# A second group by seven products in half of the gate and up units, with shared products in the accumulators' banks and 4 KB landing tiles

## The chip, the cores and the metric

The kernel runs on one core of a Trainium2 chip. The metric is the device time of one execution in microseconds. TensorE (PE) multiplies, PEld is its weight load, VectorE (DVE) and ScalarE (ACT) do the elementwise work, GpSimd (POOL) issues a few transfers, and SyncE (SP) issues the large ones.

## The reference

One layer of a decoder block on 256 tokens of width 2048, all in float32:

```
h = h + 0.5 * swiglu(rms_norm(h, ffn1_norm), ffn1_w_gate, ffn1_w_up, ffn1_w_down)
n = rms_norm(h, mix_norm) @ w_in                  # split among retention and sliding-window attention
h = h + concat(retention(n), swa(n)) @ w_out
h = h + memory_cross_attention(rms_norm(h, xa_norm), rms_norm(mem, mem_norm), xa_wq, xa_wkv, xa_wo)
h = h + 0.5 * swiglu(rms_norm(h, ffn2_norm), ffn2_w_gate, ffn2_w_up, ffn2_w_down)
out = rms_norm(h, final_norm)
swiglu(x, g, u, d) = (silu(x @ g) * (x @ u)) @ d   # g, u: 2048 x 5632; d: 5632 x 2048
```

## The kernel before

The 256 tokens are two halves t of 128, which are the rows of a matmul. The hidden width of an FFN, 5632, is 11 blocks b of 512 columns, in three groups (0 to 3, 4 to 7, 8 to 10); after the gate and up blocks of a group comes its part of the down projection. The contraction of 2048 is four groups of 512, each of four slices of 128.

**Precision.** A weight piece of float32 lands by SP's queue in a tile `wf`. ACT copies it into its high half `wh` (line 74), DVE subtracts to get the low half `wl` (line 79), both in fp32r, and PE multiplies three times (`three`, lines 632 to 634): high by high, high by low, low by high. There are four buffers each of `wh` and `wl`. The left operands (`blk`) are split in the same way.

**Units.** `Unit` is a plain product of one block. `Twin` does two outputs together: gate b and up b, or two blocks of a down projection. Three of its four contraction groups are multiplied plainly, in steps of two slices for each output (both token halves: 12 matmuls of 512 columns a step). The fourth group, `seven`, is done by seven products in place of eight, in the manner of Strassen and Winograd: token halves by outputs by halves of the contraction. A product is two slices, 6 matmuls. For it DVE subtracts weights from one another (line 222), four times a Twin, and the left operand needs sums, which `sums_of` makes for gate and up after gate b=0 is done: ACT scales four pieces of h, DVE makes four sums of 256 columns (line 279), and these are split into halves (line 74 on ACT, line 79 on DVE). There are 28 Twins: b=1 to 10 in each FFN and four for the down projections of each.

Before, four of the seven products stand alone in the four `tmp` banks of PSUM and three go into the accumulators `acc` (two tiles of two banks). One product is put behind each of the plain steps 2 to 8 of the Twin's own. DVE then adds products and accumulators in SBUF (`t2k`, line 249, eight adds a Twin).

**Order.** `later(delay, fn)` puts a task in a list by a step counter; `run_due` runs those due ahead of a step. Splits are issued LOOKAHEAD = 3 steps ahead and loads AHEAD = 4 steps before these. A scheduler orders the instructions of an engine, and each engine works in its order. Waits between engines are set by tile. Loads go to five `wf` tiles of 8 KB per partition, mostly 1 MB each.

Of the kernel before, what the change touches and what calls it, by code (L numbers as in the profile page):

```python
# [35 lines left out]
SWA_EVERY = 5  # L36


@with_exitstack
def decoder_block(ctx: ExitStack, tc: tile.TileContext, a: dict, out: bass.AP):  # L40
# [20 lines left out]
    def big(dt=F32):  # L61
        return wpool.tile([P, 2, 1024], dt, tag="wf", name=nm("wf"), bufs=5)
# [95 lines left out]
    class Unit:  # L158
# [4 lines left out]
        def __init__(self, w, index, n, lhs, done, blocks, per_half=False, pair=False):  # L163
            self.w, self.n, self.lhs, self.done = w[2 * index : 2 * index + 2] if pair else w[index], n, lhs, done
            self.blocks, self.per_half, self.pair = list(blocks), per_half, pair
            self.then = None
            units.append(self)

        def steps(self):
# [9 lines left out]
    class Twin:  # L179

        then, n, per_half = None, 512, False

        def __init__(self, weights, lhs, plain, seven, sums, done, pair=True):
            self.w, self.lhs, self.plain, self.seven = weights, lhs, list(plain), seven
            self.sums, self.done, self.pair = sums, done, pair
            self.acc, self.products, self.wide = [None, None], {}, []
            units.append(self)

        def steps(self):
            plain = [(b, f, i) for b in self.plain for f in range(2) for i in range(2)]  # L190
            out = []
            for at, (b, f, i) in enumerate(plain):
                out.append((self, b, range(2 * i, 2 * i + 2), f, b == plain[0][0] and i == 0, b == plain[-1][0] and i == 1))
                if 2 <= at < 9:
                    out.append((self, self.seven, None, at - 2, False, False))
            return out

        def fetch(self, at, steps, loaded):
            _, b, ks, f, _, _ = steps[at]
            if ks is None:  # L200
                return
            other = next(i for i in range(at + 1, len(steps)) if steps[i][2] is not None)
            loaded[at], loaded[other] = load_pair(self.w[f], b) if self.pair else load(self.w[f], 2 * b, 2)
            if b == self.plain[0]:
                self.load_wide(f)

        def load_wide(self, f):
            x, c = big(), self.seven
            if self.pair:
                nc.sync.dma_start(x, self.w[f][:, c].rearrange("f p n -> p f n"))  # L210
                x = x.rearrange("p f (k n) -> p k f n", n=S)
            else:
                nc.sync.dma_start(x, self.w[f][2 * c : 2 * c + 2].rearrange("c p n -> p c n"))
                x = x.rearrange("p c (k f n) -> p (c k) f n", k=2, f=2)
            self.wide.append(x)

        def prepare(self, kind):
            (g0, g1), (u0, u1) = ([x[:, i::2] for i in range(2)] for x in self.wide)
            src = (g0, g1, u1, g0, u0, u1, g1)[kind]
            if kind > 2:  # L220
                p, q = ((u0, g0), (u1, u0), (u1, g0), (g1, u1))[kind - 3]
                nc.vector.tensor_tensor(src, p, q, ALU.subtract)  # L222
            wh, wl = (wpool.tile([P, 1024], F32R, tag=x, name=nm(x)) for x in ("wh", "wl"))
            halves(*(x.rearrange("p (k f n) -> p k f n", k=2, f=2) for x in (wh, wl)), src)
            return [x.rearrange("p (k n) -> p k n", n=512) for x in (wh, wl)]

        def multiply(self, kind, wh, wl):
            x, sums = self.lhs[self.seven], self.sums[self.seven]
            alone = kind in (0, 3, 4, 5)
            if alone:  # L230
                o = self.products[kind] = tmp_ps()
            else:
                o = self.acc[kind == 2][:, int(kind == 6), :]
            for j in range(2):
                if kind in (0, 1, 6):
                    k, t = 2 * j + (kind > 0), int(kind == 6)
                    v = [x[:, k, c, t * P : (t + 1) * P] for c in range(2)]
                else:
                    i = {2: 3, 3: 0, 4: 2, 5: 1}[kind]
                    v = [sums[:, c, i, j, :] for c in range(2)]  # L240
                three(o, *v, wh[:, j, :], wl[:, j, :], alone and j == 0, alone and j == 1)
            if kind == 0:
                later(1.5, self.first_copy)
            if kind == 5:
                later(1, self.first_sums)
                later(2, self.second_sums)

        def add(self, out, a, b):
            nc.vector.tensor_tensor(out, a, b, ALU.add)  # L249
# [1055 lines left out]
```

## Time and profile before

| | before |
|---|---|
| median of 3 runs | 2148.33 us (2145.35 to 2149.93) |
| the profiled execution | 2148.38 us, span 2146.2 us, mean granted clock 0.997 |
| PE | 2129.7 us busy, 99% |
| DVE | 1664.5 us, 78% |
| ACT | 1144.4 us, 53% |
| transfers | 478 issues on SP's queue; 482.50 MB in all, 225 GB/s |

A row of the timeline has the start, the duration, the engine, the line, what is written and read, the shape and the count, and in brackets the idle time before it with what ended it. A matmul's row is longer than its distance from the next, since matmuls overlap. FFN1 ends at about 730 us of the span and FFN2 begins at about 1450 us; between them lie the mixer and the attention over the memory.

### The profile page before, as it was taken

The page shows a single profiled execution, that of the slowest core. Times are in us where ns is not written, and L with a number is a line of the kernel's source. Part 1 is how long each engine was busy: PE and PEld are TensorE (multiplying, and loading weights), DVE is VectorE, ACT ScalarE, POOL GpSimd, SP SyncE. Part 2 cuts the span into 40 slices and gives each one's busy share as a digit, 9 for nine tenths or more (in the row PEclk, how much of TensorE's full clock was granted, in tenths as well). Part 3 has the DMA queues.
Part 4 walks back from the last instruction along what each step waited for, and adds up shares of the span by engine and source line. Part 5 has one row for each costly group of instructions (what it writes and reads, how often), then busy time and mean ns, then how long its engine had stood idle before and what let it go on. Part 6 is the DMA issues. An engine that isn't in the chain of part 4 may idle for free.

```text
span 2146.2 us, 25612 instructions
## 1 busy us (share of the span) xinstructions
PE 2129.7 (99%) x9624; PEld 1764.9 (82%) x9624; DVE 1664.5 (78%) x1984; ACT 1144.4 (53%) x1395; POOL 159.1 (7%) x273
## 2 busy tenths in 40 slices
PE   9999999999999999999999999999999999999998
PEld 7888888888888878888788888888888888888886
DVE  6988888888885778787665555567988888888875
ACT  6555555555554554646455444455655455555554
POOL 0000100001001110101110110010100000000000
PEclk9999999999999999999999999999999999999999
DMA  7767676767657666666776766476876575656663
GB/s 295 238 205 253 233 239 224 246 218 253 230 202 255 216 225 207 204 208 221 251 249 214 241 218 206 156 245 235 250 269 225 178 249 203 233 200 228 205 227 141
DMA packets 138444, 482.50 MB, mean 225 GB/s; under 512 B 11984, under 2 KB 11984, under 8 KB 138192
## 3 DMA queue, kind: packets, MB, share of 16 engines
q1 hardware_dynamic: 125888, 447.26, 59.7%
q0 software_dynamic: 12288, 33.57, 6.7%
q8 instruction: 75, 1.23, 0.2%
q14 instruction: 49, 0.40, 0.1%
q10 hardware_dynamic: 144, 0.05, 0.0%
HBM read 445.17 MB, written 35.65 MB: 224 GB/s over the span
## 4 chain that ended last, share of the span: by engine, by line
PE 57%; DVE 2%; DMA 2%; issue 1%; ACT 0%; POOL 0%; POOLq 0%; ACTq 0%; DVEq 0%
PE acc L633 17%; PE acc L632 17%; PE acc L634 17%; DMA t4k<-box 2%; PE tmp L634 2%; PE tmp L632 2%; PE tmp L633 2%; DVE wl L79 1%; DVE h L647 0%; PE tmp L866 0%; POOL t4k L619 0%; DVE t4k L610 0%; PE tmp L847 0%; DVE blk L520 0%; DMA box<-t4k 0%
## 5 line engine op out<-in xcount | busy, mean ns | idle before, releaser
L74 ACT ACTIVATE wh<-wf 128x1024 fp32r<-128x1024 f32 (+1 forms) x861 | 905.9, 1056 | 884.5 <-PE acc L634 819.5
L79 DVE TENSOR_TENSOR wl<-wf,wh 128x1024 fp32r<-128x1024 f32 (+1 forms) x861 | 1037.9, 1215 | 373.4 <-ACT wh L74 357.6
L632 PE MATMUL acc<-wh,blk 128*128 128x512 f32 (+1 forms) x2832 | 1100.6, 389 | 1.2 <-ACT wh L74 1.2
L633 PE MATMUL acc<-wl,blk 128*128 128x512 f32 (+1 forms) x2832 | 1099.1, 388 | 1.1 <-DVE wl L79 1.0
L634 PE MATMUL acc<-wh,blk 128*128 128x512 f32 (+1 forms) x2832 | 1098.1, 388 | 0.0
L632 PEld LDWEIGHTS acc<-wh,blk 128*128 128x128 f32 x2832 | 533.0, 188 | 112.2 <-ACT wh L74 2.4
L633 PEld LDWEIGHTS acc<-wl,blk 128*128 128x128 f32 x2832 | 533.0, 188 | 109.0 <-DVE wl L79 1.9
L634 PEld LDWEIGHTS acc<-wh,blk 128*128 128x128 f32 x2832 | 532.9, 188 | 108.7
L619 POOL DMA_DIRECT2D t4k<-box x256 | 147.8, 584 | 1772.3 <-DMA box<-t4k 748.4
L222 DVE TENSOR_TENSOR wf<-wf,wf 128x1024 f32<-128x1024 f32 x84 | 102.6, 1222 | 1.9
L632 PE MATMUL tmp<-wh,blk 128*128 128x512 f32 x224 | 87.1, 389 | 0.0
L633 PE MATMUL tmp<-wl,blk 128*128 128x512 f32 x224 | 87.1, 389 | 0.0
L634 PE MATMUL tmp<-wh,blk 128*128 128x512 f32 x224 | 87.1, 389 | 0.0
L249 DVE TENSOR_TENSOR t2k<-t2k,acc 128x512 f32<-128x512 f32 x112 | 71.8, 683 | 9.5 <-PE acc L634 9.5
L249 DVE TENSOR_TENSOR t2k<-t2k,tmp 128x512 f32<-128x512 f32 x112 | 76.5, 684 | 1.9
L610 DVE STREAM_TRANSPOSE t4k<-t2k 128x512 f32<-128x512 f32 x96 | 63.0, 691 | 10.2 <-ACT t2k L74 10.0
L634 PEld LDWEIGHTS tmp<-wh,blk 128*128 128x128 f32 x224 | 42.0, 188 | 8.7
L632 PEld LDWEIGHTS tmp<-wh,blk 128*128 128x128 f32 x224 | 42.0, 188 | 8.7
L633 PEld LDWEIGHTS tmp<-wl,blk 128*128 128x128 f32 x224 | 42.0, 188 | 8.7
L79 DVE TENSOR_TENSOR blk<-t4k,blk 128x512 fp32r<-128x512 f32 (+2 forms) x72 | 44.1, 653 | 4.8 <-ACT blk L74 4.6
L74 ACT ACTIVATE blk<-t4k 128x512 fp32r<-128x512 f32 (+2 forms) x72 | 39.2, 596 | 7.5 <-DMA t4k<-box 7.5
L647 DVE TENSOR_TENSOR h<-h,t4k 128x512 f32<-128x512 f32 x40 | 25.8, 687 | 16.6 <-DMA t4k<-box 16.6
(149 smaller groups left out, 720.1 us busy)
## 6 DMA issues: line engine op xcount, KB each, us to landing
wf<-in_ffn_w_up SPq DMA_DIRECT2D x88, 1024.0 KB, 6.6
wf<-in_ffn_w_down SPq DMA_DIRECT2D x88, 1024.0 KB, 6.9
wf<-in_ffn_w_gate SPq DMA_DIRECT2D x87, 1024.0 KB, 6.9
box<-t4k SPq DMA_DIRECT2D x64, 512.0 KB, 3.3
t4k<-box POOLq DMA_DIRECT2D x256, 128.0 KB, 7.0
wf<-in_w_in_rqk SPq DMA_DIRECT2D x16, 1024.0 KB, 7.4
wf<-in_w_in_rvg SPq DMA_DIRECT2D x16, 1024.0 KB, 5.4
wf<-in_w_out SPq DMA_DIRECT2D x16, 1024.0 KB, 8.0
```

The lines of the kernel that those rows point to most:

```text
L74: return nc.scalar.activation(dst, src, AF.Copy, **kw)
L79: nc.vector.tensor_tensor(lo, src, hi, ALU.subtract)
L222: nc.vector.tensor_tensor(src, p, q, ALU.subtract)
L249: nc.vector.tensor_tensor(out, a, b, ALU.add)
L610: nc.vector.transpose(z[:, t, :].rearrange("p (g q j) -> p q g j", g=4, q=4), squares_of(v))
L619: nc.gpsimd.dma_start(z[32 * g : 32 * g + 32].rearrange("p t (i n) -> p (t i) n", i=4), far[g])
L632: nc.tensor.matmul(o, ah, bh, start=start, stop=False)
L633: nc.tensor.matmul(o, ah, bl, start=False, stop=False)
L634: nc.tensor.matmul(o, al, bh, start=False, stop=stop)
L647: nc.vector.tensor_tensor(v, v, out[t], ALU.add)
```

## The change

`Twin` is written anew.

- `sevens` takes the place of `seven`: for b in DOUBLE = (2, 4, 6, 8, 10) two of the four contraction groups (2 and 3) are done by seven products each, so two plain groups are left; in the other Twins one.
- All products accumulate in the four banks that become the Twin's outputs, the plain steps after them in the same banks. The first, third, fifth Twin of an FFN and so on takes the four `tmp` banks (`spare`), every second one the two `acc` tiles. What two outputs share is copied out of a bank by ACT (`keep`, `keep_other`, `middle`, `spread`: four copies) and added into the banks by DVE (four adds).
- A Twin that is `ahead`, all but the first of an FFN, has its products P1, P5, P6, P3 and P7 inside the preceding unit and P2 and P4 inside its own. The first (b=1) has P1, P5, P6, P3, P2 and P7 ahead of its plain steps.
- After gate b=0 `sums_of` makes the sums of block 3 (delay 1) and of block 2 (delay 8).
- `wf` is ten tiles of 4 KB per partition (`land`), one load of 512 KB each. A load of gate and up pieces brings two runs of 2 KB per partition.
- The tables and keys that lie in such tiles (`dmat`, `box`, `keys`) take two or one of the small ones.

In counts of the two programs: 60 matmuls of 512 columns fewer on PE; on DVE 30 weight splits and 40 subtractions of weights more and net 112 adds of 512 columns fewer; on ACT 30 splits and net 84 pieces of 512 columns more; on SP 863 issues in place of 478.

```diff
+LAND = 10
+DOUBLE = (2, 4, 6, 8, 10)
+P1, P5, P6, P3, P7, P2, P4 = range(7)
-    def big(dt=F32):
-        return wpool.tile([P, 2, 1024], dt, tag="wf", name=nm("wf"), bufs=5)
+    def land(dt=F32):
+        return wpool.tile([P, 1024], dt, tag="wf", name=nm("wf"), bufs=LAND)
...
     class Twin:
+        plan = {
+            P1: ((0, 0), (0, 0), (0, 0)),
+            P5: ((1, 0), (1, 1), 0),
+            P6: ((1, 0), (0, 1), 1),
+            P7: ((0, 0), (0, 1), 2),
+            P2: ((0, 1), (0, 0), (1, 0)),
+            P4: ((0, 1), (0, 1), (1, 1)),
+            P3: ((1, 1), (1, 0), 3),
+        }
...
+        def chunks(self, kinds):
+            return [
+                (self, c, None, kind, c == self.sevens[0], c == self.sevens[-1]) for kind in kinds for c in self.sevens
+            ]
...
+        def bank(self, f, t):
+            if self.spare:
+                if (f, t) not in self.acc:
+                    self.acc[f, t] = tmp_ps()
+                return self.acc[f, t]
+            if f not in self.acc:
+                self.acc[f] = ps_acc.tile([P, 2, 512], F32, tag="acc", name=nm("acc"))
+            return self.acc[f][:, t, :]
...
+            if last and kind in (P1, P5, P6, P7):
+                later(0, {P1: self.keep, P5: self.keep_other, P6: self.middle, P7: self.spread}[kind])
...
+        def keep(self):
+            self.u1 = self.copied(self.bank(0, 0))
+        def keep_other(self):
+            self.p5 = self.copied(self.bank(1, 1))
+        def middle(self):
+            x = self.bank(0, 1)
+            self.add(x, self.u1, x)
+            self.u2 = self.copied(x)
+            self.add(self.p5, self.p5, self.u2)
+        def spread(self):
+            for x, y in ((self.copied(self.bank(0, 1)), self.bank(1, 1)), (self.p5, self.bank(1, 0))):
+                self.add(y, x, y)
...
     def all_steps():
...
+        for (u, x), (after, _) in zip(groups, groups[1:] + [(None, None)]):
+            chunks = []
+            if isinstance(u, Twin):
+                if not u.ahead:
+                    out += u.chunks((P1, P5, P6, P3, P2, P7))
+                chunks = u.chunks((P2, P4) if u.ahead else (P4,))
+            own, n = len(chunks), len(x)
+            if isinstance(after, Twin) and after.ahead:
+                chunks += after.chunks((P1, P5, P6, P3, P7))
+            space = len(chunks) if len(chunks) > own else 2 * own
+            for at, step in enumerate(x):
+                out.append(step)
+                for i, c in enumerate(chunks):
+                    place = (2 * i + 1) * n // (2 * space)
+                    if i < own:
+                        place = min(place, n - 4)
+                    if place == at:
+                        out.append(c)
...
+    def load(w, piece):
+        wf = land()
+        if len(w.shape) == 3:
+            nc.sync.dma_start(wf, w[piece])
+            return wf
+        src = w[:, piece // 2, :, 512 * (piece % 2) : 512 * (piece % 2) + 512].rearrange("f p n -> p f n")
+        nc.sync.dma_start(wf.rearrange("p (f n) -> p f n", f=2), src)
+        return wf.rearrange("p (f k n) -> p k f n", f=2, k=2)
...
+            if b == 0:
+                for i in range(2):
+                    sums_of(norm, 3 - i, sums, 1 + 7 * i)
...
+    def twin(*args):
+        twins.append(Twin(*args, ahead=bool(twins), spare=len(twins) % 2 == 0))
```

The order shows two places.

**The first use of the sums, FFN1.** On PE before, 72 matmuls behind the end of up b=0 (`acc_23_220`), the first product that reads the sums (`blk_80_564`) follows a plain step of b=1:

```order
L632 MATMUL acc_77_530<-wh_84_588,blk_24_233 128x512
L633 MATMUL acc_77_530<-wl_85_589,blk_24_233 128x512
L634 MATMUL acc_77_530<-wh_84_588,blk_24_233 128x512
L632 MATMUL acc_83_575<-wh_88_601,blk_80_564 128x512
L633 MATMUL acc_83_575<-wl_89_602,blk_80_564 128x512
L634 MATMUL acc_83_575<-wh_88_601,blk_80_564 128x512
```

On PE now: up b=0 ends in `acc_31_235`, P1 of b=1 fills `tmp_86_555`, and P5 in `tmp_91_570` reads the sums, `blk_85_552`:

```order
L644 MATMUL acc_31_235<-wl_64_446,blk_58_414 128x512
L644 MATMUL acc_31_235<-wh_63_445,blk_58_414 128x512
L644 MATMUL tmp_86_555<-wh_66_463,blk_58_414 128x512
L644 MATMUL tmp_86_555<-wl_67_464,blk_58_414 128x512
L644 MATMUL tmp_86_555<-wh_66_463,blk_58_414 128x512 x2
L644 MATMUL tmp_86_555<-wl_67_464,blk_58_414 128x512
L644 MATMUL tmp_86_555<-wh_66_463,blk_58_414 128x512
L644 MATMUL tmp_91_570<-wh_71_489,blk_85_552 128x512
L644 MATMUL tmp_91_570<-wl_72_490,blk_85_552 128x512
```

Between the end of up b=0 and the first use of the sums there are 6 matmuls now. On DVE before, from the gating of b=0 (SCALAR_TENSOR_TENSOR) to the low half of the sums (the last row):

```order
L695 SCALAR_TENSOR_TENSOR t2k_65_489<-acc_23_220,n1_102,t2k_65_489 128x512
L695 SCALAR_TENSOR_TENSOR t2k_66_490<-acc_23_220,n1_102,t2k_66_490 128x512
L610 STREAM_TRANSPOSE t4k_71_515<-t2k_65_489 128x4x4x32
L610 STREAM_TRANSPOSE t4k_71_515<-t2k_66_490 128x4x4x32
L79 TENSOR_TENSOR wl_75_525<-wf_58_448,wh_74_524 128x1024
L279 TENSOR_TENSOR blk_73_519<-blk_73_519 128x256 x3
L79 TENSOR_TENSOR wl_79_549<-wf_67_493,wh_78_548 128x1024
L279 TENSOR_TENSOR blk_73_519<-blk_73_519 128x256
L79 TENSOR_TENSOR wl_82_572<-wf_58_448,wh_81_571 128x1024
L222 TENSOR_TENSOR wf_58_448<-wf_68_495,wf_58_448 128x2x2x256
L79 TENSOR_TENSOR blk_80_564<-blk_73_519,blk_80_564 128x1024
```

And now, with what stands directly ahead of the gating:

```order
L237 TENSOR_TENSOR wf_65_461<-wf_70_486,wf_65_461 128x2x2x256
L83 TENSOR_TENSOR wl_77_513<-wf_70_486,wh_76_512 128x1024
L698 SCALAR_TENSOR_TENSOR t2k_73_505<-acc_31_235,n1_102,t2k_73_505 128x512
L698 SCALAR_TENSOR_TENSOR t2k_74_506<-acc_31_235,n1_102,t2k_74_506 128x512
L618 STREAM_TRANSPOSE t4k_78_530<-t2k_73_505 128x4x4x32
L618 STREAM_TRANSPOSE t4k_78_530<-t2k_74_506 128x4x4x32
L83 TENSOR_TENSOR wl_82_540<-wf_75_509,wh_81_539 128x1024
L292 TENSOR_TENSOR blk_80_534<-blk_80_534 128x256 x3
L83 TENSOR_TENSOR wl_89_565<-wf_83_543,wh_88_564 128x1024
L292 TENSOR_TENSOR blk_80_534<-blk_80_534 128x256
L237 TENSOR_TENSOR wf_83_543<-wf_83_543,wf_70_486 128x2x2x256
L83 TENSOR_TENSOR blk_85_552<-blk_80_534,blk_85_552 128x1024
```

From the gating to the low half there is one split fewer; ahead of the gating stand subtractions and splits for the products.

**Where a Twin on the `acc` tiles begins, b=2 of FFN1.** On PE before, the plain steps of b=1 end in `acc_83_575` and those of b=2 begin in a fresh accumulator:

```order
L632 MATMUL acc_83_575<-wh_126_789,blk_35_312 128x512
L633 MATMUL acc_83_575<-wl_127_790,blk_35_312 128x512
L634 MATMUL acc_83_575<-wh_126_789,blk_35_312 128x512
L632 MATMUL acc_139_866<-wh_128_800,blk_15_135 128x512
L633 MATMUL acc_139_866<-wl_129_801,blk_15_135 128x512
```

Now, P7 of b=2 (it reads the sums `blk_85_552`) ends in the second bank of `acc_123_711`, and the first plain step (`blk_23_150`) writes the first bank of the same tile:

```order
L644 MATMUL acc_123_711<-wh_174_970,blk_85_552 128x512
L644 MATMUL acc_123_711<-wl_175_971,blk_85_552 128x512
L644 MATMUL acc_123_711<-wh_174_970,blk_85_552 128x512 x2
L644 MATMUL acc_123_711<-wl_175_971,blk_85_552 128x512
L644 MATMUL acc_123_711<-wh_174_970,blk_85_552 128x512
L644 MATMUL acc_123_711<-wh_177_988,blk_23_150 128x512
L644 MATMUL acc_123_711<-wl_178_989,blk_23_150 128x512
```

On ACT now, the copy of `spread`, `t2k_187_1034`, reads that tile between two splits:

```order
L78 ACTIVATE wh_177_988<-wf_165_926 128x1024
L78 ACTIVATE wh_180_1000<-wf_168_939 128x1024
L78 ACTIVATE wh_184_1022<-wf_173_961 128x1024
L78 ACTIVATE t2k_187_1034<-acc_123_711 128x512
L78 ACTIVATE wh_188_1038<-wf_176_974 128x1024
```

The copy and the plain step behind P7 are new; before, nothing read an accumulator until its unit was done.

More of the change, by code (lines that the diff above doesn't have):

```diff
@@ L1 @@
+import functools
 import math
@@ L187, in __init__ @@
+        loads = {P1: (0, 0), P5: (1, 0), P6: (1, 1), P2: (0, 1)}
+        def __init__(self, weights, lhs, plain, sevens, sums, done, ahead=False, spare=False):
+            self.w, self.lhs, self.plain, self.sevens = weights, lhs, list(plain), list(sevens)
+            self.sums, self.done, self.ahead, self.spare = sums, done, ahead, spare
+            self.acc, self.tiles = {}, {}
             units.append(self)
+        def chunks(self, kinds):
+            return [
+                (self, c, None, kind, c == self.sevens[0], c == self.sevens[-1]) for kind in kinds for c in self.sevens
+            ]
@@ L189, in steps @@
         def steps(self):
[L190 to L233, printed above, removed]
+            return [
+                (self, b, range(2 * i, 2 * i + 2), f, False, b == self.plain[-1] and i == 1)
+                for b in self.plain for f in range(2) for i in range(2)
+            ]
@@ new lines, in prepare, with multiply @@
+        def prepare(self, b, kind):
+            g0, g1, u0, u1 = (self.tiles.get((b, f, half)) for f in range(2) for half in range(2))
+            if kind in (P5, P6, P7, P4):
+                dst, p, q = {P5: (u0, u0, g0), P6: (u0, u1, u0), P7: (g0, u0, g0), P4: (g1, g1, u0)}[kind]
+                nc.vector.tensor_tensor(dst, p, q, ALU.subtract)
+            return split(self.tiles[(b, *self.plan[kind][0])], 512, 1)
+        def multiply(self, b, kind, first, last, wh, wl):
+            _, (f, t), left = self.plan[kind]
@@ L244, in multiply @@
-            if kind == 5:
-                later(1, self.first_sums)
-                later(2, self.second_sums)
+                if isinstance(left, tuple):
+                    v = [self.lhs[b][:, 2 * left[0] + j, c, left[1] * P : (left[1] + 1) * P] for c in range(2)]
+                else:
+                    v = [self.sums[b][:, c, left, j, :] for c in range(2)]
+                three(
+                    self.bank(f, t), *v, wh[:, j, :], wl[:, j, :],
+                    first and j == 0 and kind in (P1, P5, P6, P3), last and j == 1 and kind not in (P2, P4), True,
+                )
@@ L268, in sums_into, with finished @@
+        def middle(self):
[6 more added lines that the diff above has]
+                self.add(y, x, y)
+        def finished(self, f):
+            self.done(f, [self.bank(f, t) for t in range(2)])
     def sums_into(s, v):
@@ L466, in run_stream @@
                 run_until(lambda: b in u.sums)
-                u.multiply(which, *ready.pop(at))
+                u.multiply(b, which, first, last, *ready.pop(at))
                 clock[0] += 0.5
```

224 lines of the change are left out of this document (87 added, 137 removed).

## The prediction

> **What bounds the kernel now.** I read the page first, then the FFN stretches by windows, then the waits of PE.
>
> ```profile
> span 2146.2 us, 25612 instructions
> PE 2129.7 (99%) x9624; PEld 1764.9 (82%) x9624; DVE 1664.5 (78%) x1984; ACT 1144.4 (53%) x1395; POOL 159.1 (7%) x273
> q1 hardware_dynamic: 125888, 447.26, 59.7%
> L74 ACT ACTIVATE wh<-wf 128x1024 fp32r<-128x1024 f32 (+1 forms) x861 | 905.9, 1056 | 884.5 <-PE acc L634 819.5
> L632 PE MATMUL acc<-wh,blk 128*128 128x512 f32 (+1 forms) x2832 | 1100.6, 389 | 1.2 <-ACT wh L74 1.2
> ...
> 300.00:400.00 100.00, 100.00 (x443) 82.79 (x442) 88.36 (x96) 55.48 (x59) 6.90 (x12) 1.00 0.65 219
> ```
>
> PE is busy for all of 100 us in a gate and up stretch (the window's columns are length, PE, PEld, DVE, ACT, POOL, granted clock, DMA share, GB/s), and it waits 1.2 us in all before the 2832 matmuls of L632. ACT's idle time ends on PE: the splitting engines run behind PE's release of wh buffers. So the time is the number of matmuls times their distance, and whatever makes PE wait is added whole.
>
> **What is removed.** Each unit with two groups by seven products does 6 of 512 columns fewer; there are 5 in each FFN, so 60. Their price is not the 389 ns of a row, since rows overlap: 100 us hold 443, 0.226 us each, and single rows agree.
>
> ```profile
> 250.38 0.39 PE L632 MATMUL acc<-wh,blk 128*128 128x512 f32 x1
> 250.61 0.39 PE L633 MATMUL acc<-wl,blk 128*128 128x512 f32 x1
> ```
>
> 60 x 0.226 = **-13.6 us**.
>
> **What the new order adds: the first sums.** In b=1 of either FFN all products but the last now stand ahead of the plain steps. The second product, P5, reads the sums of block 3, which are only begun when gate b=0 is done. Before, 72 matmuls (16.3 us) lay between the end of up b=0 and the first use; now the 6 of P1 do (1.36 us). The chain of the sums in FFN1 and FFN2 (start, duration):
>
> ```profile
> 48.87 0.39 PE L634 MATMUL acc<-wh,blk 128*128 128x512 f32 x1
> 49.36 1.27 ACT L674 ACTIVATE t2k<-acc,n 128x512 f32<-128x512 f32 x2 [2.49 <-PE acc L634]
> 46.45 0.16 DVE L570 TENSOR_SCALAR ms<-tmp 128x2 f32<-128x2 f32 x1 [0.70 <-PE tmp L568]
> 52.75 1.40 DVE L695 SCALAR_TENSOR_TENSOR t2k<-acc,n,t2k 128x512 f32<-128x512 f32 x2
> 60.00 1.22 DVE L222 TENSOR_TENSOR wf<-wf,wf 128x1024 f32<-128x1024 f32 x1
> 61.13 1.23 DVE L79 TENSOR_TENSOR blk<-blk,blk 128x1024 fp32r<-128x1024 f32 x1
> ...
> 1480.22 1.23 DVE L79 TENSOR_TENSOR wl<-wf,wh 128x1024 fp32r<-128x1024 f32 x1 [3.99 <-ACT wh L74]
> 1482.15 1.41 DVE L695 SCALAR_TENSOR_TENSOR t2k<-acc,n,t2k 128x512 f32<-128x512 f32 x2 [0.70 <-PE acc L634]
> 1490.54 1.22 DVE L79 TENSOR_TENSOR blk<-blk,blk 128x1024 fp32r<-128x1024 f32 x1
> ```
>
> FFN1: the gate's last matmul starts at 48.87, so its slot ends at 49.10 (silu starts 0.26 later: the way from PE to ACT). Up has 12 matmuls more: 51.82; P1 ends at 53.18. From L695's start to the end of the sums' low half DVE took 62.36 - 52.75 = 9.61 us. The new order has one weight split less there (start to start 61.13 - 60.00 = 1.13): 8.5. Ahead of L695 it now has, from the ms at 46.45 on, subtraction, split, subtraction, subtraction, split, each waiting for the one before or for ACT's copy between (1.06): 5 x 1.22 + 1.06 = 7.2, so L695 starts at 46.6 + 7.2 = 53.8 and the low half ends at 62.3. Two matmuls of P5 need only the high half (0.45): 62.3 - 53.18 - 0.45 = 8.7 us.
>
> FFN2: L695 starts 0.26 after up's last slot: 1481.89; P1 ends at 1483.25. The new order puts a subtraction behind the split that ends at 1481.45, so L695 starts at 1482.6; the pieces up to the low half are as many as before (9.61): 1492.2. Five matmuls that need only the high half stand first (1.13): 7.8. Behind the low half DVE has a subtraction, a split and an add before the split that PE's next plain step needs, another 1.3. In all **+17.8** (14 if DVE makes up some, 19 if not). Late next are the copies of P1 and P5, and so the adds on their banks; ACT and DVE have no other work meanwhile.
>
> **The wait at every second Twin's start.** 14 of the 28 Twin units, every second, keep their products in the two acc tiles, two banks each. P7, the last product of the preceding unit, ends in the second bank of the gate's tile; ACT then copies that bank (`spread`), and the unit's first plain step writes the other bank of the same tile. The built program makes this step wait for the copy: its wait is for the count ACT reaches with it, since waits go by tile. Nothing stands between on PE, and it works in order. The gap is the way from PE to ACT (0.26), the copy, and the way back (0.05, from DVE's 1464.74 + 0.42 to PE's 1465.21).
>
> ```profile
> L74 ACT ACTIVATE t2k<-tmp 128x512 f32<-128x512 f32 x32 | 18.5, 579 | 0.0
> 1464.74 0.42 DVE L565 TENSOR_TENSOR t2k<-t2k 128x256 f32<-128x256 f32 x1
> 1465.21 0.61 PE L568 MATMUL tmp<-ones,t2k 128*128 128x1 f32 x4 [0.96 <-DVE t2k L565]
> ```
>
> 0.26 + 0.58 + 0.05 = 0.9 us, 14 times: **+12.6**. It can't be under 0.6 (copy and way back), 8.4 in all, and if half of the copies find ACT in the middle of a 1.06 us split it is 0.5 x 1.06 / 2 more on average, 16. I take 0.9, since the split ahead of the copy is released 12 matmuls earlier. In the other Twins each bank is a tile of its own; there 6 matmuls (1.36 us) cover the copy and I take nothing.
>
> **The clock.** Long gaps also slow what follows.
>
> ```profile
> PE tmp L568 <- DVE t2k L565: 4.3, 3, 1.8
> 730.00:740.00 10.00, 8.21 (x44) 7.38 (x43) 5.80 (x9) 3.91 (x6) 1.64 (x1) 0.83 0.62 211
> 1040.00:1050.00 10.00, 8.45 (x33) 6.65 (x32) 7.07 (x10) 3.61 (x4) 2.80 (x5) 0.83 0.59 199
> 1460.00:1470.00 10.00, 9.04 (x42) 7.26 (x41) 6.77 (x10) 5.04 (x6) 1.62 (x1) 1.00 0.79 295
> 736.00:737.00 1.00, 1.00 (x7) 1.00 (x6) 0.61 (x1) 0.00 (x0) 1.00 (x1) 0.50 0.86 348
> ```
>
> After two of the three waits for L565 (1.8 us the longest) the clock is 0.83 over 10 us, which is half for 3.4 us: 1.7 us lost each. After the third, 0.96 us, it stays 1.00. So I charge the two long stalls, 2 x 1.7 = **+3.4** (up to double), and the 0.9 us gaps nothing. The Trainium skill (TensorE: Matmul & The Clock Gate, Part 1: The HAM clock gate) has the clock fall after an idle window of about 3.4 us and come back after as long a busy one. By that rule too the sum takes two drops and none for the short gaps. The trace agrees with the 3.4 us at half, but here less than 2 us of idling were enough.
>
> **What DVE, ACT and the queues get.** DVE and ACT work only counts where it makes PE wait.
>
> ```profile
> 62.27 2.36 DVE L79 TENSOR_TENSOR wl<-wf,wh 128x1024 fp32r<-128x1024 f32 x2
> 89.28 1.28 DVE L249 TENSOR_TENSOR t2k<-t2k,acc 128x512 f32<-128x512 f32 x2
> L249 DVE TENSOR_TENSOR t2k<-t2k,tmp 128x512 f32<-128x512 f32 x112 | 76.5, 684 | 1.9
> wf<-in_ffn_w_gate SPq DMA_DIRECT2D x87, 1024.0 KB, 6.9
> wf<-in_ffn_w_gate SPq DMA_DIRECT2D x2, 512.0 KB, 4.8
> ```
>
> A DVE piece of 1024 costs 1.14 us (2.36 - 1.22), one of 512 some 0.64 (1.28 / 2). Counted in the built programs, DVE gains 30 splits and 40 subtractions and loses net 112 adds of 512 columns: 70 x 1.14 - 112 x 0.64 = +8 us over the program. The densest stretch, of a double unit's products and plain steps with seven products a group, has 17 splits and 5 subtractions (25.1) and some 10 pieces of 512 (6.4): 31.5 us under 150 matmuls, 33.9 us. So DVE stays just covered; without that cover it is 1 to 2 us a unit. ACT gains 30 splits (32 us) and net 84 pieces of 512 (49 us) on 1144: covered at 57%. SP issues 863 transfers, where 478 were, each of half the size. q1 is at 59.7% of its 16 engines; the new runs of 2 KB may cost more per byte, but even a third more is 80%. A tile can be reloaded a few us of PE ahead of its need at two places of FFN2 (4.8 us for 512 KB): 0 to 6 us. For these places and for some small DVE waits in FFN2's first units I take **+2**.
>
> **Sum.** -13.6 + 17.8 + 12.6 + 3.4 + 2 = +22.2, on the profiled execution's 2148.38 us (span 2146.2), which is the median of the runs shown (2148.33) to 0.05: 2170.6, **2171 us**. Its own range, by the ends above: 14 + 8.4 + 0 + 0 - 13.6 = +9, 2157; 19 + 16 + 6.8 + 6 - 13.6 = +34, 2183.
>
> **Rivals.**
>
> Some of the added waits are given back: behind a stall ACT and DVE are ahead, so a later gap is shorter, and the short gaps cost only what isn't idle anyway. Against: PE has no idle time to give back (100.00 of 100.00). Half of 17.8 and 12.6 and no clock: -13.6 + 15.2 = 2150, to 2157.
>
> Other side: the sums come in time. If DVE took the sums ahead of L695 and the splits, the chain would be ACT's four scalings, the four sums and the two halves, and with copies that cost PE nothing only the 13.6 us are left: 2135, to 2144. It decides from the point where the sums are ready 1.36 us behind up. Against: the order of DVE is fixed in the program and has L695, the turning and two splits first; in the trace the chain took 10 us from up's end.
>
> The 14 gaps stay away: the copy reads one bank while PE writes the other, so PE would lose nothing if it went on at once: 2171 - 12.6 = 2158. Against: the step's wait for ACT's count stands in the program. The Trainium skill (PSUM — Partial Sum Buffer, PSUM bank collisions raise a hardware error) asks for guards between engines by bank and quadrant, and by that rule this wait is not needed; no row of the trace shows the case.
>
> DVE becomes the bound in the 10 double units: 31.5 of 33.9 us is close, and one late split delays PE by its own 1.14: 10 x 1 to 2 us more, 2181 to 2191.
>
> Each of the 14 gaps drops the clock: 14 x 1.7 = 24 more, 2195. Against it the 0.96 us gap above.
>
> Transfers bind, with half the bytes in each: the densest windows have a DMA share of 0.81 (below), and there the loads would come 6 us late in sum, or 2 x 2.5 us at both places and more: 2177 to 2190.
>
> ```profile
> 1500.00:1600.00 100.00, 100.00 (x443) 82.80 (x442) 90.13 (x99) 58.17 (x63) 11.52 (x20) 1.00 0.81 263
> ```
>
> **Chances.** Forecast 0.62; waits partly given back 0.11; faster 0.05; no short gaps 0.03; DVE 0.08; clock 0.05; transfers 0.06. The range leaves out the faster case, most of the lower half of the first rival and the clock case: 2154 to 2188. 0.2% (4.3 us) is about what a measurement of this kernel can tell: faster is below 2144.0 (0.05), slower above 2152.6 (the forecast 0.62, the last four rivals 0.22, 0.07 of the first: 0.91), the same 0.04.
>
> **What would show it.** PE's waits would list two long ones at P5 (about 53 to 62 us and 1483 to 1492 from the start), for the sums' high and low half, of 8 to 9 us each; 14 of 0.9 us for ACT's copy of an acc bank, about every 85 us in a gate and up stretch; in between 100.00 of PE in 100 us and 443 matmuls. The clock would be under 1.00 behind the two long waits and nowhere else new. 60 matmuls fewer must be there. It is wrong if PE waits for DVE's splits or for wf inside the double units, if the clock falls behind the short gaps, or if the products' first use waits much less than 8 us.

## The result and the profile after

The changed kernel takes 2193.7 us (median of 4 runs, 2192.6 to 2197.5) where the kernel before took 2147.27 in the same comparison: 1.0218 times as long, 95% interval 1.0201 to 1.0236, so 46 us slower. The forecast was 2171, with a range of 2154 to 2188: the right side, but 23 us too little and outside the range.

From the page of the changed kernel:

```profile
span 2191.7 us, 26751 instructions
PE 2137.2 (98%) x9564; PEld 1753.1 (80%) x9564; DVE 1673.9 (76%) x1952; ACT 1210.9 (55%) x1519; POOL 160.2 (7%) x273
q1 hardware_dynamic: 208720, 447.28, 61.8%
wf<-in_ffn_w_gate SPq DMA_DIRECT2D x176, 512.0 KB, 5.8
wf<-in_ffn_w_up SPq DMA_DIRECT2D x176, 512.0 KB, 8.4
```

PE has 60 matmuls fewer and is still busy 7.5 us longer, since rows at half the clock (0.63 us in place of 0.39) and right behind a wait (0.50 us) are longer. The waits of PE (engine, what waits, for what; us in total, times, longest):

```profile
PE tmp L644 <- ACT blk L78: 14.4, 2, 7.8
PE tmp L644 <- DVE wl L83: 14.3, 19, 2.0
PE acc L644 <- ACT t2k L78: 9.8, 14, 0.8
PE tmp L576 <- DVE t2k L573: 2.2, 2, 1.8
```

The first and the third line are the two that the prediction asked for: two long waits for the sums and 14 short ones for ACT's copy. The second, 19 waits for splits, is what it had named as a sign of being wrong. A stretch with the largest of these and one almost without, as windows:

```profile
300.00:400.00 100.00, 95.97 (x414) 76.70 (x414) 84.79 (x87) 57.33 (x62) 4.61 (x8) 1.00 0.71 225
400.00:500.00 100.00, 99.31 (x439) 81.93 (x438) 81.56 (x82) 58.84 (x68) 5.17 (x9) 1.00 0.65 212
```

Before, each of these had 443 matmuls. In 300 to 400 there are 29 fewer, 6.6 us of PE, and DVE is busy for less of the time than before (84.8 against 88.4).

The table adds up PE's lost time from its timeline: for each row the start less the start of the row before, less 0.2267 us for each matmul of 512 columns in the earlier row, where over 0.13 us is left. So the restart behind a wait and the half clock are in it, not only the waits. FFN1 is up to 730 us, FFN2 from 1440 us on.

| lost on PE, us | before | changed |
|---|---|---|
| first sums and the half clock behind them | 0 | 11.5 + 10.0 |
| 14 copies of an `acc` bank | 0 | 6.1 + 5.9 |
| other waits in the Twins ("late") | 0 | 12.0 + 10.0 |
| norms at both FFNs' starts | 2.2 | 4.8 |
| between the FFNs | 12.8 | 8.8 |
| sum | 15.0 | 69.1 |

54.1 us more are lost and 60 x 0.227 = 13.6 are won, 40.5; the spans differ by 45.5. Of the rest 3.5 us are in gaps under 0.13 us (11.8 against 8.3) and 0.5 us in the first 45 us.

**The first sums.** DVE and PE of the changed kernel in FFN1 (timelines):

```profile
47.05 0.16 DVE L578 TENSOR_SCALAR ms<-tmp 128x2 f32<-128x2 f32 x1 [0.70 <-PE tmp L576]
50.87 2.48 DVE L237 TENSOR_TENSOR wf<-wf,wf 128x1024 f32<-128x1024 f32 x2
54.42 1.40 DVE L698 SCALAR_TENSOR_TENSOR t2k<-acc,n,t2k 128x512 f32<-128x512 f32 x2
61.74 1.23 DVE L83 TENSOR_TENSOR blk<-blk,blk 128x1024 fp32r<-128x1024 f32 x1
61.76 0.80 PE L644 MATMUL tmp<-wh,blk 128*128 128x512 f32 x1 [7.82 <-ACT blk L78]
```

The gating starts 7.37 us behind the ms (forecast 7.2) and the low half ends 8.55 us behind that (forecast 8.5).

**The short gaps.** All 14 look like this one, at 85 to 90 us from one another in a gate and up stretch:

```profile
120.93 0.50 PE L644 MATMUL acc<-wh,blk 128*128 128x512 f32 x1 [0.69 <-ACT t2k L78]
```

**The late waits.** Around the longest, at 351.85 us, the timelines of SP's queue, DVE and PE, and two windows:

```profile
321.57 0.37 SPq L362 DMA_DIRECT2D wf<-in_ffn_w_gate  x1
332.08 0.37 SPq L622 DMA_DIRECT2D box<-t4k  x1
332.54 0.42 SPq L362 DMA_DIRECT2D wf<-in_ffn_w_gate  x1
333.05 0.83 SPq L362 DMA_DIRECT2D wf<-in_ffn_w_up  x1
333.98 0.49 SPq L362 DMA_DIRECT2D wf<-in_ffn_w_gate  x1
334.52 4.77 SPq L362 DMA_DIRECT2D wf<-in_ffn_w_up  x5
```

```profile
344.97 1.22 DVE L237 TENSOR_TENSOR wf<-wf,wf 128x1024 f32<-128x1024 f32 x1 [2.52 <-DMA wf<-in_ffn_w_up]
349.43 1.23 DVE L237 TENSOR_TENSOR wf<-wf,wf 128x1024 f32<-128x1024 f32 x1 [2.10 <-DMA wf<-in_ffn_w_up]
351.85 0.50 PE L644 MATMUL tmp<-wl,blk 128*128 128x512 f32 x1 [2.01 <-DVE wl L83]
```

```profile
324.00:332.00 8.00, 8.00 (x37) 6.64 (x36) 7.97 (x11) 5.36 (x7) 0.00 (x0) 1.00 0.11 43
336.00:342.00 6.00, 6.00 (x29) 4.95 (x28) 5.95 (x6) 3.65 (x4) 2.30 (x4) 1.00 1.00 297
```

For 10 us SP's queue issues nothing: at its head stands the write of a turned block (`box`), which waits for DVE's transposes. From 324 to 332 the transfers move 43 GB/s. Then eight loads go at once, the engines are full at 297 GB/s, and the last up pieces land when DVE's subtraction has waited for them twice. DVE works in order, so a split behind that subtraction is late, and PE waits for it. In all DVE's subtractions waited 39.7 us for up weights; before, 84 of them had 1.9 us of idle time ahead of them in all, whatever ended it.

The hold itself is not new. The waits of SP's queue for DVE's transposes, in the kernel before and in the changed one:

```profile
SPq L614 <- DVE t4k L610: 586.4, 59, 20.2
...
SPq L622 <- DVE t4k L618: 606.8, 59, 26.9
```

Before, the queue was held about as long, and no row of DVE's waits was for a weight. New are what stands behind a hold (nearly twice as many loads, most of half the size, with a shorter lead in the double units) and how little room DVE has when they are late.

### The profile page after: what moved, and what is told of

It is laid out like the page before. It is cut to its first block, busy times and chain, and to the rows that moved or that the text cites. A ratio compares the mean times of both kernels' runs of the same rounds, so it can differ in the third digit from the quotient of the medians.

```text
span 2191.7 us, 26751 instructions
## 1 busy us (share of the span) xinstructions
PE 2137.2 (98%) x9564; PEld 1753.1 (80%) x9564; DVE 1673.9 (76%) x1952; ACT 1210.9 (55%) x1519; POOL 160.2 (7%) x273
## 3 DMA queue, kind: packets, MB, share of 16 engines
q1 hardware_dynamic: 208720, 447.28, 61.8%
## 4 chain that ended last, share of the span: by engine, by line
PE 54%; DVE 3%; DMA 3%; issue 1%; ACT 1%; SPq 0%; DVEq 0%; ACTq 0%; POOLq 0%; POOL 0%
PE acc L644 42%; PE tmp L644 11%; DMA wf<-in_ffn_w_up 2%; DVE wl L83 2%; DMA wf<-in_ffn_w_down 1%; PE tmp L877 0%; ACT t2k L78 0%; DVE t2k L698 0%; PE tmp L858 0%; ACT wh L78 0%; DVE t4k L618 0%; DVE tmp L255 0%; DVE blk L83 0%; PE tmp L951 0%; PE tmp L824 0%
## 5 line engine op out<-in xcount | busy, mean ns | idle before, releaser
L644 PE MATMUL acc<-wh,blk 128*128 128x512 f32 (+1 forms) x4336 | 1365.8, 389 | 10.9 <-ACT t2k L78 9.8
L644 PEld LDWEIGHTS acc<-wh,blk 128*128 128x128 f32 x4336 | 813.2, 188 | 185.4 <-ACT t2k L78 15.7
L644 PE MATMUL acc<-wl,blk 128*128 128x512 f32 (+1 forms) x2168 | 841.5, 388 | 0.8 <-DVE wl L83 0.7
L644 PE MATMUL tmp<-wh,blk 128*128 128x512 f32 x1736 | 567.5, 393 | 16.2 <-ACT blk L78 14.4
L644 PEld LDWEIGHTS acc<-wl,blk 128*128 128x128 f32 x2168 | 408.4, 188 | 83.6 <-DVE wl L83 2.8
L644 PEld LDWEIGHTS tmp<-wh,blk 128*128 128x128 f32 x1736 | 328.0, 189 | 88.5 <-ACT blk L78 15.2
L644 PE MATMUL tmp<-wl,blk 128*128 128x512 f32 x868 | 342.6, 395 | 14.5 <-DVE wl L83 14.3
L237 DVE TENSOR_TENSOR wf<-wf,wf 128x1024 f32<-128x1024 f32 x152 | 185.1, 1221 | 45.8 <-DMA wf<-in_ffn_w_up 39.7
L644 PEld LDWEIGHTS tmp<-wl,blk 128*128 128x128 f32 x868 | 164.2, 189 | 58.2 <-DVE wl L83 24.3
L618 DVE STREAM_TRANSPOSE t4k<-t2k 128x512 f32<-128x512 f32 x96 | 63.4, 691 | 12.8 <-ACT t2k L78 12.7
L78 ACT ACTIVATE t2k<-acc 128x512 f32<-128x512 f32 x72 | 42.1, 597 | 35.3 <-PE acc L644 22.6
L83 DVE TENSOR_TENSOR blk<-t4k,blk 128x512 fp32r<-128x512 f32 (+2 forms) x72 | 44.1, 653 | 10.7 <-ACT blk L78 10.5
```

Source lines behind the costliest of these rows:

```text
L78: return nc.scalar.activation(dst, src, AF.Copy, **kw)
L83: nc.vector.tensor_tensor(lo, src, hi, ALU.subtract)
L237: nc.vector.tensor_tensor(dst, p, q, ALU.subtract)
L618: nc.vector.transpose(z[:, t, :].rearrange("p (g q j) -> p q g j", g=4, q=4), squares_of(v))
L644: nc.tensor.matmul(o, x, y, start=first, stop=last, skip_group_check=shared)
```

## The experiments

The theories were: the sums, the copies and the loads each cost what the table says, and the late waits come from loads that start too late (held queue, short lead, slow runs of 2 KB). The rival for the late waits was DVE: too many splits and subtractions in the double units, whatever the loads do. All ratios are against the kernel before, measured beside. Since the runs come from several comparisons, what an edit wins is taken from the ratios, times 2147 us.

| kernel | us | ratio | 95% | sums + clock | copies | late | between |
|---|---|---|---|---|---|---|---|
| changed | 2193.7 | 1.0218 | 1.0201 to 1.0236 | 21.5 | 12.0 | 22.0 | 8.8 |
| p7_earlier | 2176.5 | 1.0136 | 1.0117 to 1.0154 | 25.0 with a norm wait | 0 | 17.2 | 8.3 |
| contiguous | 2183.3 | 1.0167 | 1.0150 to 1.0185 | 21.5 | 11.9 | 15.2 | 8.8 |
| box_on_pool | 2190.6 | 1.0200 | 1.0182 to 1.0217 | 22.6 | 12.0 | 10.7 | 17.6 |
| ahead_6 | 2179.9 | 1.0155 | 1.0134 to 1.0177 | 20.9 | 11.9 | 8.5 | 11.5 |
| plain_b1 | 2170.1 | 1.0103 | 1.0088 to 1.0118 | 0 | 11.9 | 22.1 | 11.2 |
| sums_earlier | 2188.7 | 1.0192 | 1.0176 to 1.0209 | (see there) | 12 | (see there) | 8.9 |
| no_doubles | 2185.1 | 1.0174 | 1.0154 to 1.0193 | 29.3 with a norm wait | 12 | 0.3 | 8.5 |
| all_mended | 2136.1 | 0.9947 | 0.9932 to 0.9962 | 0 | 0 | 2.2 | 9.8 |
| mended_2k_runs | 2141.3 | 0.9978 | 0.9968 to 0.9988 | 0 | 0 | 5.6 | 13.4 |
| mended_lead_8 | 2154.1 | 1.0041 | 1.0026 to 1.0057 | 0 | 0 | 7.3 | 23.1 |
| mended_nine_doubles | 2132.8 | 0.9934 | 0.9921 to 0.9948 | 0 | 0 | 6.6 | 12.1 |
| mended_no_doubles | 2148.6 | 1.0011 | 1.0001 to 1.0021 | 0 | 0 | 0.7 | 13.0 |

The last four columns are the sums of the table above, in us, from each kernel's profiled execution.

### The last shared product one step earlier

```diff
                     if i < own:
                         place = min(place, n - 4)
+                    place = min(place, n - 2)
```

> The last chunk of shared products (P7) is placed one plain step earlier, so that 12 matmuls of the preceding unit stand between it and the next unit's first step; nothing else is changed. If the 14 waits of 0.7 us for ACT's copy of an accumulator bank (0.85 us each with the restart) come from the copy standing directly behind P7, they go: 14 x 0.85 = 12 us less than the changed kernel, about 2182. If PE would be waiting for DVE or loads there anyway, the waits reappear under DVE's splits and less than 4 us are won. The waits for the first sums and for DVE's splits (14 us) should stay.

All 14 waits are gone from PE's list, 12 us as priced, and 17.6 us are won. The waits for splits by themselves went from 22.0 to 17.2, which nobody expected: DVE's subtractions still waited 37.6 us for up weights, so the loads were no earlier; with the copies and adds further from the splits a late load was absorbed more often. That last link was not tried by itself.

### One run of 4 KB per partition in FFN2

```diff
-twin([w[2 * b : 2 * b + 2] for w in (w_gate, w_up)], norm.blocks, plain, sevens, sums, done)
+ws = [w[2 * b : 2 * b + 2] if norm is n1 else w[b] for w in (w_gate, w_up)]
+twin(ws, norm.blocks, plain, sevens, sums, done)
...
+    for n in ("ffn2_w_gate", "ffn2_w_up"):
+        arrays[n] = _pieces(w[n], 512)
```

> Gate and up weights of FFN2 alone are laid out so that one load of 512 KB is one run of 4 KB per partition, in place of two runs of 2 KB; FFN1 keeps the two runs. Runs theory (2 KB runs make a burst of loads slow, so DVE's subtractions wait for up weights): the late waits in FFN2's units, 9.5 us between 1560 and 2110 us, fall to under 3 and those of FFN1 (12 us) stay: some 7 us less, about 2187. Queue theory (SP's queue is held by the write of a turned block, and the loads behind it start too late) or a DVE that is too dense: FFN2's waits stay within 2 us, 2192 to 2194.

FFN2's late waits fall from 10.0 to 3.7 us, FFN1's stay (12.0 and 11.5): within one execution the half with the longer runs loses a third of what the other does. So the length of the runs counts, as the runs theory said; 11 us are won in all.

### The turned blocks' writes on POOL's queue

```diff
-            nc.sync.dma_start(box.rearrange("(t p) n -> p t n", t=2), z)
+            nc.gpsimd.dma_start(box.rearrange("(t p) n -> p t n", t=2), z)
```

> The write of each turned block to DRAM is issued on POOL's queue in place of SP's, where it waits for DVE's transposes with all later loads behind it; the reads were on POOL's already. Queue theory: loads start when a tile is free, DVE's subtractions no longer wait 40 us for up weights, PE's 14 us of waits for splits fall under 4: 12 to 18 us less, 2176 to 2182. Runs theory: the loads are spread out but no faster, a part is won, 4 to 8 us. DVE theory (too many splits and subtractions in the double units): nothing, 2192 to 2195. If the writes are slower from that queue, the turned blocks come later and the middle of the program loses some us.

DVE's waits of the changed kernel and of this one, for up weights and for turned blocks:

```profile
DVE wf L237 <- DMA wf<-in_ffn_w_up: 39.7, 17, 4.6
DVE h L659 <- DMA t4k<-box: 4.4, 5, 1.5
...
DVE h L659 <- DMA t4k<-box: 18.4, 7, 4.0
DVE wf L237 <- DMA wf<-in_ffn_w_up: 7.0, 5, 1.8
```

With the queue free the up weights are nearly in time, and the late waits halve (22.0 to 10.7), though the queue theory had PE's waits for splits under 4. What is left is in part a new wait: DVE now waits for turned blocks, 18.4 us in place of 4.4, with splits behind. And 8.8 us more are lost between the FFNs, where PE waits for DVE's splits of turned blocks, so the kernel as a whole is only 4 us faster, where 12 to 18 were expected, and its interval overlaps the changed kernel's. The queue theory holds for the loads; as a remedy it isn't worth much.

### Loads asked for six steps ahead

```diff
-AHEAD = 4
+AHEAD = 6
```

> Loads are asked for 6 steps ahead of the splits in place of 4; a shared product counts as a step though it is half as long, so the lead in time was shorter. Lead theory: the 14 us of waits for splits halve, 7 to 10 us less, 2184 to 2187. Queue theory: the loads are still behind the same writes, but more of them are ahead of each, so some is won. DVE theory: nothing. If the ten tiles are the limit, a load waits for its tile at the head of the queue and nothing is won either, 2192 to 2195.

13.5 us are won, more than the lead theory gave: late waits fall from 22.0 to 8.5 and those of DVE for up weights from 39.7 to 16.1 (for all weights of the FFNs from 42.8 to 29.9). The DVE theory, which gave nothing for this run and the two before it, falls as a cause that stands alone: DVE had the same work in all of them. That a dense DVE is needed as well shows below (no double units).

### b=1 without products

```diff
-                    sevens = (2, 3) if b in DOUBLE else (3,)
+                    sevens = () if b == 1 else (2, 3) if b in DOUBLE else (3,)
```

(The first plain step then opens the banks.)

> The first Twin of each FFN (b=1) does all four groups plainly, 12 matmuls more in the program (2.7 us); its products and so the early use of the sums are gone, and the sums are first read some 25 us later. If the two long waits (7.8 and 6.6 us) and the half clock behind them come from the sums being read 6 matmuls after up b=0, all of the 21.5 us there go: 2193.7 - 21.5 + 2.7 = 2175. If the clock or DVE would lose as much elsewhere, less than 10 us are won. The 14 waits for ACT's copy and the late waits stay.

The 21.5 us are gone, the norm's wait at FFN2's start is back at 0.5 us as well (4.1 in the changed kernel), and 25 us are won for 12 matmuls. The waits for the copies and the late waits are what they were (11.9, 22.1).

### Sums begun earlier

```diff
             if b == 0:
-                for i in range(2):
-                    sums_of(norm, 3 - i, sums, 1 + 7 * i)
+                sums_of(norm, 2, sums, 8)
...
+        if norm is n1:
+            sums_of(norm, 3, sums, 12)
+        else:
+            st["sums2"] = lambda: sums_of(norm, 3, sums, 0.5)
```

(`st["sums2"]` is called when the last block of h is there.)

> The sums of block 3 are begun as soon as the block is there, not when gate b=0 is done; the products stay where they are. If the start of the chain is what is late, the waits for the sums go, and what is left in the first Twin is DVE's work for six products in a row (9 pieces of 1.14 and 4 of 0.64 us, 12.8, under 36 matmuls, 8.2 us): 3 to 5 us a Twin, so some 12 us won, 2181. If DVE and ACT have no room for the sums ahead of the gate's end (they run through the norm there), gate and up b=0 wait instead and less than 5 us are won.

Only 6 us are won. No wait for the sums is left, but PE waits in the same place for what comes next. PE of this kernel in FFN1's first Twin:

```profile
60.46 0.50 PE L644 MATMUL tmp<-wl,blk 128*128 128x512 f32 x1 [2.00 <-DVE wl L83]
68.32 1.15 PE L644 MATMUL tmp<-wh,blk 128*128 128x512 f32 x2 [1.55 <-ACT wh L78]
```

In FFN1 the late sum is 17.9 us in place of 12.0, 5.9 in the first Twin; in FFN2 it is 20.0 in place of 10.0, and the norm's wait grew to 3.2 us, with half the clock behind it. (That wait was 0.8 to 4.3 us in other kernels that keep the late sums, so it isn't shown to come from this edit.) Six products in a row need more of DVE (12.8 us by its rows) than PE takes for them (8.2), and DVE had no room ahead of the gate's end either: in FFN1 its gating began 2.3 us later (56.69 us against 54.42), where up ended 1.1 us later. So the row of products seems to count as much as the start of the chain; making room for both, as plain_b1 does, wins more.

### No double units

```diff
-DOUBLE = (2, 4, 6, 8, 10)
+DOUBLE = ()
```

> No unit has a second group by seven products: 60 matmuls more (13.6 us); products in the banks, their order and the 4 KB landing tiles stay. If the late waits (22 us) come from the double units alone, where products without loads stand close and loads and subtractions with them, they fall under 6: 2193.7 + 13.6 - 16 = 2191. If the landing tiles and the short lead are enough to make them in every unit, they stay: 2205 to 2208. The waits for the sums (21) and for ACT's copy (12) stay by either.

PE's waits of this kernel have no line for splits:

```profile
PE tmp L644 <- ACT blk L78: 14.4, 2, 7.8
PE acc L644 <- ACT t2k L78: 9.8, 14, 0.8
PE tmp L576 <- DVE t2k L573: 5.0, 2, 4.3
...
PE acc L644 <- ACT wh L78: 1.0, 1, 1.0
```

The late waits are down to 0.3 us, though the tiles of 4 KB, the runs of 2 KB and the lead are those of the changed kernel. DVE still waits for weights here:

```profile
DVE wf L237 <- DMA wf<-in_ffn_w_up: 16.0, 11, 2.5
DVE wf L237 <- DMA wf<-in_ffn_w_down: 13.3, 5, 3.9
```

That is 29.3 us, where the changed kernel has 42.8 (39.7 and 3.1) and loses 22.0 on PE, and ahead_6 has 29.9 and loses 8.5; here PE loses next to nothing. So the late waits need both: loads that come late, and double units, in which DVE has no room to make them up. Those units save 13.6 us of matmuls and lost 22 by waits: without them the change is 9 us faster (1.0174 against 1.0218). FFN2's norm waited longer here (4.3 us).

### All of it mended

p7_earlier, plain_b1 and ahead_6 together, and the longer runs for every load of gate, up and down weights.

```diff
-AHEAD = 4
+AHEAD = 6
...
+                    place = min(place, n - 2)
...
-                    sevens = (2, 3) if b in DOUBLE else (3,)
+                    sevens = () if b == 1 else (2, 3) if b in DOUBLE else (3,)
...
+    for n in ("ffn2_w_gate", "ffn2_w_up", "ffn1_w_down", "w_out", "xa_wo"):
+        arrays[n] = _pieces(w[n], 512)
```

(The gate and up weights of FFN1 from b=1 on are laid out so too.)

> b=1 plain, P7 one plain step earlier, loads asked for 6 steps ahead, and every load of gate, up and down weights one run of 4 KB per partition; the double units stay. If the waits found so far are all that the change lost, PE is again without waits in both FFNs: 48 matmuls fewer than before (10.9 us), 2147 - 11 = 2136, with 2 to 6 us for late waits that are left: 2138 to 2142. If DVE is too dense in the double units once loads are in time, 1 to 2 us a unit stay: 2146 to 2156.

```profile
span 2133.5 us, 26701 instructions
PE 2119.5 (99%) x9576; PEld 1753.9 (82%) x9576; DVE 1653.0 (77%) x1930; ACT 1201.5 (56%) x1505; POOL 158.8 (7%) x273
```

```profile
PE acc L645 <- DVE wl L83: 2.8, 2, 2.0
PE tmp L101 <- POOL ident masks.py:199: 1.4, 1, 1.4
PE acc L645 <- ACT wh L78: 1.0, 1, 1.0
```

```profile
300.00:400.00 100.00, 100.00 (x441) 82.16 (x440) 90.97 (x95) 62.35 (x71) 4.62 (x8) 1.00 0.65 211
```

2136.1 us: a ratio of 0.9947, so 11 us less than the kernel before and 58 us less than the changed one. In 300 to 400 us PE is full again, with DVE at 91%: the same double units with the same splits and subtractions, and no wait. DVE waited 4.9 us for up weights in this kernel, so with the loads in time the density of DVE alone costs little (2.2 us of late waits).

### Four kernels from there

The 2 KB runs put back:

```diff
-    for n in ("ffn2_w_gate", "ffn2_w_up", "ffn1_w_down", "w_out", "xa_wo"):
-        arrays[n] = _pieces(w[n], 512)
+    for n in ("ffn1_w_gate", "ffn1_w_up", "ffn1_w_down", "w_out", "xa_wq", "xa_wo", "ffn2_w_gate", "ffn2_w_up"):
+        arrays[n] = _pieces(w[n], 256)
```

> As all_mended, but the loads of gate, up and down keep their two runs of 2 KB per partition; loads are asked for 6 steps ahead. If the length of the runs slows a burst whatever the lead, half of the late waits come back, 5 to 9 us: 2141 to 2145. If a lead of two steps more covers slower loads, at most 3 us: 2136 to 2139.

The 2 KB runs cost 6.7 us even with the longer lead (late 5.6 in place of 2.2, between the FFNs 13.4 in place of 9.8), as the runs theory said.

A longer lead:

```diff
-AHEAD = 6
+AHEAD = 8
```

> As all_mended, with loads asked for 8 steps ahead. If the lead was still what is left (2 us of late waits), 1 to 2 us less: 2134 to 2136. If ten tiles are the limit, nothing, or a load that waits for its tile holds the writes of turned blocks behind it on the same queue and some us are lost: 2136 to 2141.

20 us slower than all_mended. SP's queue (what waits, for what; us, times, longest) in all_mended and here:

```profile
SPq L360 <- DVE wl L83: 996.3, 461, 8.0
...
SPq L360 <- DVE wl L83: 1269.3, 567, 12.2
```

Ten tiles are the limit: a load waits for its tile up to 12.2 us at the head of the queue, what stands behind it is late, and 13 us more are lost between the FFNs (23.1 against 9.8). It was far worse than the few us expected.

More double units, and none:

```diff
-DOUBLE = (2, 4, 6, 8, 10)
+DOUBLE = tuple(range(2, 11))
```

> As all_mended, with two groups by seven products in every unit from b=2 on (18 in place of 10): 48 matmuls fewer (10.9 us), and 8 units more with 3 splits and 4 subtractions of DVE more each. By the estimate of 31.5 us of DVE under 33.9 us of PE in a double unit DVE is still covered, and it is faster: 2125 to 2128. If a row of such units with the turning and gating between them is over DVE's capacity, PE waits for splits by 0.5 to 2 us a unit and the gain is gone: 2132 to 2142.

2132.8 us, the lowest here (0.9934), but by 3 us where 48 matmuls are 10.9, and the intervals of the two overlap: 4.4 us more are lost in the Twins and 2.3 between the FFNs. The longest wait in a Twin is not for DVE but for ACT's copy of a bank, behind four splits in a row on ACT:

```profile
1604.37 0.50 PE L645 MATMUL acc<-wh,blk 128*128 128x512 f32 x1 [1.64 <-ACT t2k L78]
```

The others are under 0.5 us each, for splits and halves by DVE and ACT. So the gain is gone for the most part, as the second case of the expectation said, but that DVE is what is short in a row of such units is not shown.

```diff
-DOUBLE = (2, 4, 6, 8, 10)
+DOUBLE = ()
```

> As all_mended, with one group by seven products in every unit: 60 matmuls more (13.6 us). If all_mended is bound by PE everywhere, 2136 + 13.6 = 2150; if its double units still lost some us, less than that: 2145 to 2148.

2148.6 us, 13.7 above all_mended by the ratios, where 60 matmuls are 13.6: with loads in time the double units are worth what they save. Without them the kernel is 1.0011 times the one before, 2.4 us, and its b=1 has 12 matmuls more than that one (2.7 us): all the rest of the change wins nothing and costs nothing.

## Why the prediction was right and wrong

- **The matmuls.** 60 x 0.226 = 13.6 us. Right: 9564 rows in place of 9624, and mended_no_doubles gives 13.7 for these 60.
- **The first sums**, 17.8 us, and **the clock**, 3.4. Right in place and chain, and plain_b1 takes them away. The sum is right in part by luck: 11.5 + 10.0 = 21.5 us against 21.2, but the two waits were 7.8 and 6.6 us, 14.4 together and so 3.4 less than priced, and the clock was half for 6.2 and 5.6 us after PE had begun again, not 3.4 each. That is 5.9 us lost in place of 3.4, and the rest is restarts and short waits right behind. The two errors nearly cancel.
- **The wait at every second Twin's start**, 14 x 0.9 = 12.6. Right: 14 x 0.86 = 12.0, none of which dropped the clock; p7_earlier takes them away. The rival without these gaps falls.
- **What DVE, ACT and the queues get**, +2. This is the step that failed. It was sized by the landing time of a load (4.8 us), by the mean share of q1 and by two places of FFN2. What the runs showed in its place is 22.0 us of late waits: 20 of the 23 us that were missed. The rest is the norms' 2.6, the small gaps' 3.5 and 4.0 less between the FFNs. The step did not follow SP's queue: the written block was in it (as it was before, without cost), 10 us of nothing behind it and then a burst that the engines need some 14 us for (an estimate: eight loads, 4.2 MB at 297 GB/s). And it counted the lead in steps, though a shared product is half a step long, and takes four loads for seven products: in a double unit the same seven steps ahead are a shorter time. q1's share was 61.8%, well under the 80% allowed, and says nothing on it: a mean hides a queue that is held and then full.
- **The transfers as a rival** came nearest: loads that are late, and a time of 2177 to 2190. But it had them some 6 us late in sum, where 22.0 us were lost, at places of FFN2 alone, where the waits are in both FFNs, and a chance of 0.06.
- **DVE as the bound** falls as the whole cause for ten double units: at 91% of a stretch PE had no wait in all_mended. The estimate of 31.5 us under 33.9 (93%) was good. But so dense a DVE can't make up a late load, and without the double units late loads cost 0.3 us: half of this rival is in the cause. For 18 such units it stays open (mended_nine_doubles).
- **Waits partly given back** falls: the long waits came to 14.4 us of the 17.8 priced and the 14 short ones to 12.0 of 12.6, far from half.
- **The other side** falls too: the sums came 7.8 us late. With the causes taken away the forecast of that rival (2135 for the matmuls alone) is near where all_mended ends, 2136, which has 48 matmuls fewer, not 60.

Not forecast were two smaller things: FFN2's first norm waited 1.8 us for DVE in place of 1.0 and dropped the clock (4.1 us in place of 1.6), and between the FFNs PE lost 4 us less, since two waits for a norm that had dropped the clock before (730 to 740 and 1040 to 1050 us) were shorter now. What moved them was not tried.

What stays open is how the late waits divide among the held queue, the runs and the lead: each remedy alone takes 7 to 13 us of the 22 (the longer runs in one FFN alone), so they overlap, and the late waits of p7_earlier fell by 5 with loads no earlier.

## What to carry to other kernels

Before a change makes the work of the engines that feed the bound one denser, follow the queue that feeds them in its own order: what waits at its head, how long it is empty and how full the burst behind that is. A mean share of 60% was no cover, and a hold that cost nothing before was part of 22 us together with later loads and denser work. Shared work that is put right behind its own inputs, or an accumulator copied right ahead of the next write to its tile, costs the whole way there and back each time; with 12 matmuls between the product and that write the 14 waits were gone. And a lead counted in steps shrinks when the steps do.

## What the runs showed of the hardware

The length of a gap didn't decide alone whether the clock fell. In the changed kernel a gap of 2.01 us at 351.85 us left it at full rate, while one of 1.83 us at 1486.69 was followed by half the clock:

```profile
352.00:354.00 2.00, 2.00 (x9) 1.65 (x10) 2.00 (x2) 0.88 (x2) 0.00 (x0) 1.00 0.60 215
1486.69 0.61 PE L576 MATMUL tmp<-ones,t2k 128*128 128x1 f32 x4 [1.83 <-DVE t2k L573]
1488.00:1490.00 2.00, 2.00 (x6) 1.57 (x5) 0.64 (x1) 0.00 (x0) 1.22 (x1) 0.50 0.09 34
60.00:68.00 8.00, 6.20 (x14) 4.42 (x15) 4.25 (x6) 3.34 (x5) 2.47 (x4) 0.50 0.98 260
1513.10:1518.60 5.50, 5.50 (x13) 3.99 (x14) 3.39 (x3) 1.50 (x3) 2.33 (x4) 0.50 1.00 315
```

Behind the long wait of FFN1 the clock was half for 6.2 us after PE had begun again (61.8 to 68), and behind that of FFN2 for 5.6 us (1513.1 to 1518.7), not 3.4. The Trainium skill (TensorE: Matmul & The Clock Gate, Part 1: The HAM clock gate) has windows of about 3.4 us that run freely, whatever the kernel does; the trace agrees. Its records of the granted clock change at 57.76, 68.00, 1487.94, 1491.36, 1511.84 and 1518.66 us, and each of these times lies a whole multiple of 3.413 us from the first, to 0.01 us; the changes in the other 13 traces lie on such a grid too. On the changed kernel's grid the gap of 1.83 us lies in one window, and that of 2.01 us is cut into 1.47 and 0.54.

In the 14 traces every window at full rate with 1.96 us or more of idle PE was followed by half the clock, and none with under 1.5. In between both occurred (1.55 us in the kernel before was, 1.91 in the changed one was not), so where the limit lies, and whether it is idle time alone, stays open.

In the burst above, loads in two runs of 2 KB filled the engines at 297 GB/s (share 1.00, with the reads of turned blocks beside them). That is not the most such loads can move; in the same kernel:

```profile
72.00:76.00 4.00, 4.00 (x19) 3.31 (x18) 3.73 (x5) 2.40 (x3) 0.00 (x0) 1.00 1.04 386
```

What made the difference is not shown. Doubling the run cut the late waits of the FFN that had it by 6 us at the same number of bytes (10.0 to 3.7).
